# A two-layer hybrid diffusion step on one core: order of transposes, products, weight loads and output tiles changed

## The chip, the cores and the metric

One core of a Trainium2 chip runs the whole step. TensorE (PE, with its weight loads shown as PEld) multiplies and transposes, VectorE (DVE), ScalarE (ACT) and GpSimd (POOL) do the rest, and SyncE (SP) issues most of the transfers; ACT issues some. Each engine takes its own instructions in order. The metric is the device time of one execution in microseconds, lower is better.

## The reference: what is computed

Two layers are applied to 256 context tokens and to 1024 latent tokens of width 1024. A layer normalises and modulates its input, projects it to 4400 columns, runs three groups of heads over it in both directions, and projects the result back:

```python
h = _rmsnorm(x, g) * (1.0 + scale) + shift
proj = jnp.einsum('bld,de->ble', h, w_in)
# A: mLSTM, 4 heads x 128      ya = sigmoid(ao) * (ha_f + flip(ha_b))
# B: retention, 4 heads x 64   yb = hb_f + flip(hb_b)
# C: gated linear attention    yc = hc_f + flip(hc_b)
y = jnp.concatenate([_head_rms(ya), _head_rms(yb), _head_rms(yc)], axis=-1)
y = y * hn_g * jax.nn.silu(jnp.concatenate([az, bz, cz], axis=-1))
out = jnp.einsum('ble,ed->bld', y, w_out)
x = x + gate * out
```

Shift, scale and gate come from a modulation, a product of a vector with w_ada. Latent scans start from cached states; the final states of the context scans are returned as well as both outputs.

## The kernel before

The 1280 tokens are ten chunks of 128, in three blocks of 256, 512 and 512 tokens (BLK). Every large product is done in three terms: inputs and weights are each split in a high part, ACT's cast (L516), and a low part, DVE's subtraction (L517), and hi*hi, hi*lo and lo*hi are accumulated, 24 matmuls for a block or a chunk. The split inputs stay in hA (blocks 0 and 1) and hB (block 2).

Weights are loaded on SP's queue into a ring of two raw tiles (L526, in load), and split into rings of three hi and three lo tiles. Loads and splits are traced ahead of their use by a scheduling priority (AHEAD); load adds an order behind the fourth last entry of a list of past projections (uses). A feature-major projection (mm_fm, L566) takes one tile of 512 KB and goes over the three blocks; a token-major one (mm_tm, L581) takes two tiles and goes over the chunks in pairs. Results go through two PSUM banks (pj). A layer has 22 feature-major projections (14 of ORDER, eight gate paths) and nine token-major ones (five of ORDER, four of the output). gates (L702) is a product of its own, with three weight pieces of 304 columns (gates_w); the third piece of layer 0 is loaded into a tile of the arena f.

The order of PE's work is written by a planner (Weave). Each stage is a generator, which yields a gap, a condition and the tiles it needs; the planner takes the first that is ready by its own clock and costs, and chains PE's instructions in that order. So a PE instruction that waits holds back all behind it. Threads run in the order of rank: the mixers, then the modulations, then the projections of ORDER, then the fillers (gate paths, gate_z). The other engines' order comes from a scheduler that simulates times.

The parts that the change and the prediction touch:

- late_setup and decay_setup (L318 to L342) load masks, gate biases, initial maxima and the retention decays (L335, L338), and take a log-sigmoid of the decays (L310 to L316) before the planned part begins. load_x (L458) loads tokens.
- modulation_late computes one quarter of a modulation: eight products (L418), ACT's copy of the row (L422), a fold (L427) 4 us later by the planner's clock.
- group_c: for five pairs of chunks it transposes keys (L1007), multiplies them with the values into one bank, two products for each chunk (L1015), and updates states with DVE (L987, L991) after each chunk's products.
- head_a, one mLSTM head: for pairs of chunks it loads rows (rows_in, L1485) and prepares weights (L1494 to L1497); in each step come products (L1510, L1512), then the next pair's scores (L1503) with DVE's multiply (L1504) in the first half of the bank `other`, then transposes of the output of two steps earlier (L1551) in its second half, and the head's arithmetic (L1518 to L1574). Steps are 5 us apart by the planner.
- gate_z multiplies a group's output by its gate path: it loads a tile of yd (L1591), projects (L566), and writes yd back (L1597), through wk, a ring of three tiles.
- fillers: when the last gate path is to be done, two f tiles take block 0 of the seven other output tiles (L1627). The entry z of ORDER then waits for the gate paths and, in layer 0, for the modulations (early).
- out_proj: for all three blocks it loads tiles of yd through wk (L1693), splits them (L1694, L1695), allocates ten xt tiles, transposes the gate vector (L1701), writes it to DRAM (grow) and reads it back broadcast (L1709), loads the ten x chunks (L1712), and runs four token-major products, whose evictions (L1725) take a wk tile each.

The arena f has 12 tiles. `edge` with SCHED_ONLY and `issue_after` order instructions without a semaphore.

Of the kernel before, what the change touches and what calls it, by code (L numbers as in the profile page):

```python
# [9 lines left out]
F32 = mybir.dt.float32  # L10
# [81 lines left out]
def hybrid_step(ctx: ExitStack, tc: tile.TileContext, A, O):  # L92
# [225 lines left out]
    def late_setup():  # L318
        t = rw()
        sync.dma_start(t, A["cst"][:, K_MF:K_MF + 4 * P])  # L320
        dve.tensor_copy(masks, t)
        dve.tensor_scalar(later, t[:, 0:P], 0.0, None, ALU.is_lt)
# [8 lines left out]
    def decay_setup():  # L331
# [5 lines left out]
        for t in range(2):  # L337
            sync.dma_start(lg[64 * t:64 * t + 64, 16:24], rl2[t:t + 1, :].to_broadcast([64, 8]),  # L338
                           allow_slow_non_contiguous=True)

# [65 lines left out]
    def modulation_late(l, c0):  # L406
# [17 lines left out]
        yield wait(4.0, mx=1)  # L424
# [25 lines left out]

    def load_x(b):
# [59 lines left out]
    def split(raw, parts=1, cols=1024):  # L511
        hi, lo = hi_ring(), lo_ring()
        n = cols // parts
        for i in range(0, cols, n):
            e = slice(i, i + n)
            act.copy(hi[:, e], raw[:, e])  # L516
            dve.tensor_tensor(lo[:, e], raw[:, e], hi[:, e].bitcast(F32), ALU.subtract)  # L517
        return hi, lo

    anchor, uses = [None], []  # L520

    def load(*dmas):

        with ExitStack() if anchor[0] is None else tc.issue_after(anchor[0]):
            for out, src in dmas:
                i = sync.dma_start(out, src)  # L526
                if len(uses) > 4:
                    edge(i.ins, uses[-4], mybir.DependencyReason.SCHED_ONLY)

    def w_fm(src, c0):  # L530

        with tc.high_priority(offset=AHEAD):
            raw = raw_ring()
            load((v3(raw, P), src[:, c0:c0 + P].rearrange("(k p) n -> p k n", p=P)))
            hi, lo = split(raw)
        return v3(hi, P), v3(lo, P)

    def w_tm(src, c0, ks=range(KT)):

        out = []  # L540
        for g in range(2):
            with tc.high_priority(offset=AHEAD):
                raw = raw_ring()
                i = 0
                while i < 4:
                    k = ks[4 * g + i]
                    n = 1
                    while i + n < 4 and ks[4 * g + i + n] == k + n:
                        n += 1
                    load((v3(raw, 256)[:, i:i + n, :],  # L550
                          src[k * P:(k + n) * P, c0:c0 + 256].rearrange("(k p) n -> p k n", p=P)))
                    i += n
# [1305 lines left out]
```

## Time and profile before

| | us |
|---|---|
| median of 2 timed runs | 1773.28 (1768.79 to 1777.78) |
| the profiled execution's own time | 1782.73 |
| its span, first to last instruction | 1780.9 |
| PE busy | 1607.7 (90%), 11126 matmuls |
| DVE busy | 889.8 (50%) |
| ACT busy | 608.1 (34%) |
| POOL busy | 116.5 (7%) |
| moved by DMA | 239.64 MB, 135 GB/s on average |

An engine's busy time is the union of its instructions. Idle time of PE is put down to what ended it. The mean granted clock of PE is 0.949 of full speed; it is either 1 (2.4 GHz) or 0.5 (1.2 GHz).

### The profile page before, as it was taken

What the parts mean: (1) busy time and instruction counts of PE and PEld (TensorE: products, weight loads), DVE (VectorE), ACT (ScalarE), POOL (GpSimd) and SP (SyncE); (2) the same over time, 40 slices, a digit from 0 to 9 for tenths busy, and PEclk for the clock granted to TensorE, in tenths of its full rate; (3) what the DMA queues carried; (4) which work ended last, traced back from release to release, by engine and by line L of the source; (5) the groups of instructions that cost most, each with busy time, mean ns of one, the idle gap of its engine ahead of it and who ended that gap; (6) DMA issues with size and microseconds to landing.
All of it is one profiled execution on the core that took longest, in us unless ns stands there. A gap on an engine that the chain in (4) does not pass through costs nothing.

```text
span 1780.9 us, 28991 instructions
## 1 busy us (share of the span) xinstructions
PE 1607.7 (90%) x11126; PEld 1455.8 (82%) x11126; DVE 889.8 (50%) x2216; ACT 608.1 (34%) x1553; POOL 116.5 (7%) x195
## 2 busy tenths in 40 slices
PE   6698899999999877897999988999999989888897
PEld 3577689998988766786999868999899877776897
DVE  3449444572354454544354785347505455554545
ACT  5454213112433332233255631221224333323323
POOL 1100010101000000000011000110100000000001
PEclk8799999999999988997999999999999999898799
DMA  8134326424647466553131331271244546566303
GB/s 315 53 113 126 100 99 219 119 63 133 187 139 217 134 190 208 175 174 119 38 113 48 111 105 58 95 237 51 77 144 141 164 124 209 164 192 195 96 13 121
DMA packets 217409, 239.64 MB, mean 135 GB/s; under 512 B 23901, under 2 KB 171645, under 8 KB 217261
## 3 DMA queue, kind: packets, MB, share of 16 engines
q1 hardware_dynamic: 179392, 195.68, 36.2%
q10 hardware_dynamic: 37868, 42.01, 6.8%
q8 instruction: 89, 1.46, 0.3%
q14 instruction: 60, 0.48, 0.1%
HBM read 173.01 MB, written 64.55 MB: 133 GB/s over the span
## 4 chain that ended last, share of the span: by engine, by line
PE 41%; DMA 7%; DVE 5%; ACT 2%; issue 1%; SPq 1%; POOL 0%; ACTq 0%; POOLq 0%; DVEq 0%
PE pj L581 18%; PE pj L566 14%; DMA yd<-wk 2%; DMA wk<-yd 2%; PE pj L702 2%; DMA rw<-wrow 1%; DMA rw<-rrow 1%; PE mx L1449 1%; DMA f<-sp 1%; PE mx L1510 1%; PE mx L1512 1%; DVE f L659 1%; DVE lo L517 1%; PE mx L1315 1%; PE mx L1078 0%
## 5 line engine op out<-in xcount | busy, mean ns | idle before, releaser
L566 PE MATMUL pj<-hA,hi 128*128 128x256 f32 (+1 forms) x1408 | 364.5, 351 | 10.9 <-ACT wk L594 10.7
L581 PE MATMUL pj<-hi,hA 128*128 128x256 f32 x1728 | 338.0, 296 | 23.0 <-ACT hA L1694 12.9
L581 PEld LDWEIGHTS pj<-hi,hA 128*128 128x128 f32 x1728 | 283.0, 200 | 30.6 <-ACT hA L1694 15.7
L566 PEld LDWEIGHTS pj<-hA,hi 128*128 128x128 f32 x1408 | 245.3, 196 | 43.1 <-ACT wk L594 11.1
L581 PE MATMUL pj<-lo,hA 128*128 128x256 f32 x864 | 251.6, 291 | 0.0
L566 PE MATMUL pj<-hA,lo 128*128 128x512 f32 (+1 forms) x704 | 242.3, 344 | 0.0
L566 PE MATMUL pj<-hB,hi 128*128 128x512 f32 x704 | 229.4, 408 | 11.4 <-DVE wk L1595 10.5
L581 PE MATMUL pj<-hi,hB 128*128 128x256 f32 x1152 | 212.2, 285 | 0.0
L517 DVE TENSOR_TENSOR lo<-raw,hi 128x256 fp32r<-128x256 f32 (+2 forms) x193 | 116.4, 624 | 153.2 <-ACT hi L516 134.9
L581 PEld LDWEIGHTS pj<-hi,hB 128*128 128x128 f32 x1152 | 179.0, 191 | 1.6 <-issue 0.8
L581 PEld LDWEIGHTS pj<-lo,hA 128*128 128x128 f32 x864 | 173.3, 201 | 0.0
L566 PEld LDWEIGHTS pj<-hB,hi 128*128 128x128 f32 x704 | 132.7, 195 | 41.4 <-DVE wk L1595 11.3
L581 PE MATMUL pj<-lo,hB 128*128 128x256 f32 x576 | 162.9, 283 | 0.0
L516 ACT CAST hi<-raw 128x256 fp32r<-128x256 f32 (+2 forms) x193 | 104.5, 565 | 139.6 <-PE pj L566 98.6
L566 PEld LDWEIGHTS pj<-hA,lo 128*128 128x128 f32 x704 | 137.2, 195 | 15.9
L566 PE MATMUL pj<-hB,lo 128*128 128x512 f32 x352 | 141.0, 401 | 0.0
L581 PEld LDWEIGHTS pj<-lo,hB 128*128 128x128 f32 x576 | 110.2, 191 | 0.0
L444 ACT ACTIVATE rw<-f 128x256 bf16<-128x256 f32 (+1 forms) x90 | 43.4, 484 | 123.1 <-DVE f L1728 121.5
L592 ACT COPY wk<-pj 128x256 f32<-128x256 f32 (+1 forms) x102 | 40.9, 431 | 126.5 <-PE pj L581 63.8
L566 PEld LDWEIGHTS pj<-hB,lo 128*128 128x128 f32 x352 | 68.1, 193 | 15.4
L1725 DVE TENSOR_TENSOR wk<-pj,f 128x512 f32<-128x512 f32 (+1 forms) x45 | 28.4, 632 | 95.5 <-PE pj L581 95.5
L1441 ACT ACTIVATE sm<-mx,ccol 128x128 f32<-128x128 f32 x144 | 45.9, 367 | 65.0 <-PE mx L1438 63.9
(271 smaller groups left out, 2426.8 us busy)
## 6 DMA issues: line engine op xcount, KB each, us to landing
raw<-in_w_in_dram SPq DMA_DIRECT2D x64, 512.0 KB
f<-in_w_ada_dram SPq DMA_DIRECT2D x48, 512.0 KB
f<-sp SPq DMA_DIRECT2D x36, 640.0 KB
sp<-wk ACTq DMA_DIRECT2D x128, 128.0 KB
wk<-yd SPq DMA_DIRECT2D x64, 256.0 KB
sp<-wk ACTq DMA_DIRECT2D x56, 256.0 KB
rw<-rrow SPq DMA_DIRECT2D x40, 256.0 KB
rw<-wrow SPq DMA_DIRECT2D x40, 256.0 KB
```

The source lines that it names most:

```text
L444: act.activation(rw().bitcast(BF16)[:, 0:x.shape[1]], x, AF.Square, accum_out=out)
L516: act.copy(hi[:, e], raw[:, e])
L517: dve.tensor_tensor(lo[:, e], raw[:, e], hi[:, e].bitcast(F32), ALU.subtract)
L566: end = pe.matmul(ps[:, :n], lhsT=w[wi][:, k, :], rhs=hblk(xi, k, b), start=(i == 0), stop=(i == 23))
L581: end = pe.matmul(pv[:, u, :], lhsT=hchunk(xi, k, c), rhs=w[e // 4][wi][:, e % 4, :], start=(i == 0), stop=(i == 23))
L592: act.copy(out, ps)
L659: dve.tensor_tensor_scan(o, ones[r, 0:n], i, 0.0, ALU.mult, ALU.add)
L702: end = pe.matmul(ps, lhsT=hchunk(xi, k, c), rhs=w[k // 3][wi][:, k % 3, :], start=(i == 0), stop=(i == 23))
L1315: pe.matmul(banks[u][:, (2 * d + r) * P:(2 * d + r + 1) * P], lhsT=last[d][:, (2 * u + r) * P:(2 * u + r + 1) * P], rhs=vv[r][:, c, 0:P], ...
L1441: act.activation(ks[:, d * P:(d + 1) * P], pk, AF.Copy, scale=ccol[:, c, 2 + d, hd:hd + 1])
L1449: pe.matmul(U[d], lhsT=ks[:, d * P:(d + 1) * P], rhs=v[:, c, :], start=True, stop=True)
L1725: dve.tensor_tensor(t, pv, row.unsqueeze(1).to_broadcast([P, len(cs), 256]), ALU.mult)
```

## The change

late_setup becomes a thread of the planner that takes in decay_setup: its loads come after the last x load, and masks and log-sigmoid 20 and 40 us later. The modulation's fold waits 8 us for 4. load makes raw tile, load and split in one; loads are ordered behind the end of the projection two back (for the last gate piece, one back), splits behind the middle of the projection before; token-major tiles are split in two parts for four; the third gate piece uses the raw ring. In group_c all four products of a step come before the updates; in head_a the transposes come before the scores. In fillers the last gate path waits for 12 free f tiles and, in layer 0, for the modulations, and then out_tiles loads blocks 0 and 1 of the seven output tiles, the gate vectors and six x chunks; out_proj loads the rest.

```diff
     def late_setup():
-        t = rw()
+        yield wait()
+        t = rw.take()
         sync.dma_start(t, A["cst"][:, K_MF:K_MF + 4 * P])
-        dve.tensor_copy(masks, t)
-        dve.tensor_scalar(later, t[:, 0:P], 0.0, None, ALU.is_lt)
...
-    def decay_setup():
...
+        yield wait(20.0)
+        dve.tensor_copy(masks, t)
+        dve.tensor_scalar(later, t[:, 0:P], 0.0, None, ALU.is_lt)
+        rw.give(t)
+        yield wait(20.0)
         lt = sm()
         log_sigmoid(lg, lt[:, 0:24], lt[:, 24:48])
...
-        yield wait(4.0, mx=1)
+        yield wait(8.0, mx=1)
...
-            sync.dma_start(t, tokens(A["x_prompt"], A["x_sample"], c0 + j))
+            xl.append(sync.dma_start(t, tokens(A["x_prompt"], A["x_sample"], c0 + j)))
...
+    def load(src, *parts, behind=2, n=1):
         hi, lo = hi_ring(), lo_ring()
+        raw = raw_ring()
+        with tc.high_priority(offset=AHEAD):
+            with ExitStack() if anchor[0] is None else tc.issue_after(anchor[0]):
+                for view, rows in parts:
+                    i = sync.dma_start(view(raw), rows)
+                    if len(ends) >= behind:
+                        edge(i.ins, ends[-behind], mybir.DependencyReason.SCHED_ONLY)
+            for j in range(0, src, src // n):
+                c = slice(j, j + src // n)
+                for i in (act.copy(hi[:, c], raw[:, c]),
+                          dve.tensor_tensor(lo[:, c], raw[:, c], hi[:, c].bitcast(F32), ALU.subtract)):
+                    if mids and behind > 1:
+                        edge(i.ins, mids[-1], mybir.DependencyReason.SCHED_ONLY)
         return hi, lo
...
-            for out, src in dmas:
-                i = sync.dma_start(out, src)
-                if len(uses) > 4:
-                    edge(i.ins, uses[-4], mybir.DependencyReason.SCHED_ONLY)
...
-        if b == 2:
-            uses.append(end.ins)
+        if b:
+            (ends if b == 2 else mids).append(end.ins)
...
-        if cs[-1] == NCH - 1:
-            uses.extend([end.ins] * 2)
+        if cs[-1] in (5, NCH - 1):
+            (mids if cs[-1] == 5 else ends).append(end.ins)
...
-            raw = f5(1024) if l == 0 and k == 6 else raw_ring()
...
+            hi, lo = load(n * 304, *parts, behind=1 if k == 6 else 2)
...
                 for u, c in enumerate(order[i - 1]):
+                    for p in range(2):
+                        h = slice(256 * u + p * P, 256 * u + (p + 1) * P)
+                        pe.matmul(bank[:, h], lhsT=last[:, h], rhs=v3(vt[p], 129)[:, c, 0:P], start=True, stop=True)
+                for u, c in enumerate(order[i - 1]):
                     U = bank[:, 256 * u:256 * u + 256]
...
-            if ahead:
-                scores(c0 + 2, ahead[0], other[:, 0:256])
             out = before.pop(0) if len(before) == 2 or before and c0 >= NCH else None
             if out is not None:
                 was, pt = out[1], other[:, 256:512]
                 for u in range(2):
                     pe.transpose(pt[:, u * P:(u + 1) * P], out[0][:, u * P:(u + 1) * P], ident)
+            if ahead:
+                scores(c0 + 2, ahead[0], other[:, 0:256])
...
-                    yield wait(0, f=2)
...
+                    yield wait(0, cond=early, f=12, mx=1, sm=1)
+                    e["y"] = out_tiles(l, [kt for kt in range(KT) if kt not in tiles_of[g]])
...
-                yield wait(0, cond=lambda: not left and not busy and "y" in e and early())
+                yield wait(0, cond=lambda: not left and not busy and "y" in e)
...
+    def out_tiles(l, kts):
         xt = [f5(1280) for _ in range(NCH)]
+        first = [f5(1280) for _ in range(2)]
+        y = {}
+        for i, kt in enumerate(kts):
+            y[0, kt] = first[i // 5][:, 256 * (i % 5):256 * (i % 5) + 256]
+            y[1, kt] = xt[6 + i // 2][:, 512 * (i % 2):512 * (i % 2) + 512]
+        for b, kt in sorted(y):
+            t0, n = BLK[b]
+            sync.dma_start(y[b, kt], yd[kt, :, t0:t0 + n])
...
-        sync.dma_start(grow, gr)
+        act.dma_start(grow, gr)
...
+        for c in range(6):
+            x_in(l, c, xt[c])
+        return xt, first, gate, y
+
+    def out_proj(l, tiles, normed):
+
+        xt, first, gate, y = tiles
...
+        f5.give(*first)
+        for c in range(6, NCH):
+            x_in(l, c, xt[c])
...
-            with tc.issue_after(adas[-1].ins):
-                late_setup()
...
+            weave.add(late_setup())
+            with tc.issue_after(xl[-1].ins):
+                weave.visit(weave.threads[0])
```

## Rows read from the trace of the kernel before

**Rows 1.** Busy us by stretch: length, PE, PEld, DVE, ACT, POOL; clock; DMA share; GB/s

```profile
0.00:80.00 80.00, 47.93 (x274) 32.70 (x275) 34.02 (x63) 43.32 (x80) 12.52 (x31) 0.81 0.60 205
...
160.00:240.00 80.00, 63.56 (x387) 53.01 (x386) 48.27 (x114) 22.49 (x44) 3.55 (x3) 0.94 0.32 98
...
500.00:790.00 290.00, 251.41 (x1556) 219.41 (x1555) 139.42 (x433) 95.22 (x281) 17.01 (x36) 0.92 0.58 177
790.00:830.00 40.00, 27.56 (x138) 23.84 (x137) 17.43 (x30) 13.85 (x31) 0.20 (x1) 0.70 0.57 168
...
1380.00:1630.00 250.00, 215.85 (x1302) 191.01 (x1301) 132.39 (x405) 86.15 (x264) 15.56 (x29) 0.94 0.56 173
1630.00:1672.00 42.00, 31.46 (x160) 27.48 (x159) 18.75 (x34) 13.92 (x30) 0.00 (x0) 0.72 0.51 154
```

**Rows 2.** Waits of PE: who waited for whom, us in total, times, longest

```profile
PE mx L1551 <- DVE rw L1504: 42.8, 16, 7.1
PE pj L581 <- ACT hA L1694: 12.9, 10, 2.4
PE pj L702 <- DVE lo L517: 12.6, 2, 12.1
...
PE mx L427 <- ACT wk L422: 11.0, 1, 11.0
PE pj L566 <- DVE wk L1595: 10.5, 3, 5.4
PE mx L1015 <- DVE f L991: 9.3, 8, 2.2
...
PE pj L581 <- DVE wk L1725: 8.1, 2, 4.2
```

**Rows 3.** Timeline at the start, 40 to 64 us: start, us, engine, line

```profile
46.73 1.65 SPq L526 DMA_DIRECT2D f<-in_w_in_dram  x2
...
48.94 1.42 SPq L338 DMA_DIRECT2D lg<-in_ret_decay_logit_dram  x2
...
50.59 0.88 PE L702 MATMUL pj<-hi,hA 128*128 128x304 f32 x2 [5.07 <-ACT hi L516]
61.65 0.18 DVE L310 SCALAR_TENSOR_TENSOR sm<-lg 128x24 f32<-128x24 f32 x1 [11.64 <-issue]
...
63.60 0.62 PE L702 MATMUL pj<-lo,hA 128*128 128x304 f32 x1 [12.13 <-DVE lo L517]
```

**Rows 4.** Timeline of a head stage, 583 to 606 us

```profile
587.68 0.69 DVE L1497 TENSOR_TENSOR rw<-rw,f 128x512 f32<-128x512 f32 x1 [3.48 <-DMA rw<-wrow]
...
589.09 0.69 PE L1551 MATMUL mx<-cst,sm 128*128 128x128 f32 x2 [4.96 <-DVE rw L1504]
...
600.40 0.44 PE L1551 MATMUL mx<-cst,sm 128*128 128x128 f32 x2 [0.86 <-DVE rw L1504]
```

**Rows 5.** Busy time by stretch, behind the long wait

```profile
589.00:594.50 5.50, 5.41 (x17) 4.55 (x18) 2.00 (x8) 2.22 (x9) 0.70 (x1) 0.50 0.35 111
```

**Rows 6.** Timeline of the output projection's start, layer 0: PE, SP, DVE

```profile
793.77 0.48 PE L581 MATMUL pj<-hi,hA 128*128 128x256 f32 x2
...
805.27 17.19 SPq L1693 DMA_DIRECT2D wk<-yd  x11
...
839.08 0.69 DVE L1725 TENSOR_TENSOR wk<-pj,f 128x512 f32<-128x512 f32 x1 [4.27 <-PE pj L581]
...
844.84 0.69 DVE L1725 TENSOR_TENSOR wk<-pj,f 128x512 f32<-128x512 f32 x1 [0.69 <-PE pj L581]
```

**Rows 7.** Line L427, all its instructions: duration min/median/max, first and last start

```profile
L427 PE MATMUL mx<-fold,wk x64: 165/251/371, 132.3 to 697.1; 128*128 128x2 f32 x64
```

**Rows 8.** Waits of SP's queue, the first line

```profile
SPq L526 <- DVE lo L517: 361.5, 34, 40.3
```

**Rows 9.** Timeline, 620 to 637 us: a weight tile's split on ACT and DVE

```profile
626.16 1.03 ACT L516 CAST hi<-raw 128x1024 fp32r<-128x1024 f32 x1
...
627.24 1.22 DVE L517 TENSOR_TENSOR lo<-raw,hi 128x1024 fp32r<-128x1024 f32 x1
```

More of the change, by code (lines that the diff above doesn't have):

```diff
@@ L449, in rstd @@
         pool.tensor_tensor(ss, ss, mhalf[:, 0:ss.shape[1]], ALU.pow)
+    xl = []
     def load_x(b):
@@ L508, in norm_thread @@
         done.add(b)
-    def split(raw, parts=1, cols=1024):
+    anchor, mids, ends = [None], [], []
+    def load(src, *parts, behind=2, n=1):
         hi, lo = hi_ring(), lo_ring()
[L513 to L517, printed above, removed]
-        return hi, lo
-    anchor, uses = [None], []
-    def load(*dmas):
-        with ExitStack() if anchor[0] is None else tc.issue_after(anchor[0]):
-            for out, src in dmas:
-                i = sync.dma_start(out, src)
-                if len(uses) > 4:
-                    edge(i.ins, uses[-4], mybir.DependencyReason.SCHED_ONLY)
+        raw = raw_ring()
[11 more added lines that the diff above has]
+                        edge(i.ins, mids[-1], mybir.DependencyReason.SCHED_ONLY)
+        return hi, lo
     def w_fm(src, c0):
[L532 to L535, printed above, removed]
+        hi, lo = load(1024, (lambda t: v3(t, P), src[:, c0:c0 + P].rearrange("(k p) n -> p k n", p=P)))
         return v3(hi, P), v3(lo, P)
@@ L541, in w_tm @@
         for g in range(2):
[L542 to L552, printed above, removed]
-                hi, lo = split(raw, 4)
+            parts, i = [], 0
+            while i < 4:
+                k = ks[4 * g + i]
+                n = 1
+                while i + n < 4 and ks[4 * g + i + n] == k + n:
+                    n += 1
+                parts.append((lambda t, i=i, n=n: v3(t, 256)[:, i:i + n, :],
+                              src[k * P:(k + n) * P, c0:c0 + 256].rearrange("(k p) n -> p k n", p=P)))
+                i += n
+            hi, lo = load(1024, *parts, n=2)
             out.append((v3(hi, 256), v3(lo, 256)))
@@ L667, in gates_w @@
             n = min(3, KT - k)
-            raw = f5(1024) if l == 0 and k == 6 else raw_ring()
-            r = v3(raw[:, 0:912], 304)[:, 0:n, :]
-            load(*[(r[:, :, d:d + m], src[:, k:k + n, c0:c0 + m])
-                   for d, c0, m in ((0, C_CV, 256), (256, C_AG, 16), (272, C_LR, 32))])
-            hi, lo = split(raw, 1, n * 304)
-            if l == 0 and k == 6:
-                f5.give(raw)
+            parts = [(lambda t, d=d, m=m: v3(t[:, 0:912], 304)[:, 0:n, d:d + m], src[:, k:k + n, c0:c0 + m])
+                     for d, c0, m in ((0, C_CV, 256), (256, C_AG, 16), (272, C_LR, 32))]
+            hi, lo = load(n * 304, *parts, behind=1 if k == 6 else 2)
             out.append((v3(hi[:, 0:912], 304), v3(lo[:, 0:912], 304)))
@@ L715, in gates @@
             pend.append((c, gt))
-        uses.extend([end.ins] * 3)
+            if c in (5, NCH - 1):
+                (mids if c == 5 else ends).append(end.ins)
         def rest():
@@ L1784, in program @@
         if not general:
-            with tc.issue_after(adas[-1].ins):
-                late_setup()
-        if not general:
-            with tc.issue_after(adas[-1].ins):
-                decay_setup()
+            weave.add(late_setup())
+            with tc.issue_after(xl[-1].ins):
+                weave.visit(weave.threads[0])
         anchor[0] = None if general else adas[-1].ins
-        uses.clear()
+        for marks in (mids, ends):
+            marks.clear()
         normed, prepared = set(), set()
```

42 lines of the change are left out of this document (15 added, 27 removed).

## The prediction, as put on record before the result was known

> **What bounds the kernel now.** I read the stretches first, then the waits of PE, then the timeline around each long wait, and last SP's waits. The stretches [rows 1] show that PE is the bound, but not everywhere alike: from 0 to 80 us it is busy for 47.9 us at a granted clock of 0.81, from 160 to 240 for 63.6, in the mLSTM head stages (500 to 790 and 1380 to 1630) for 251.4 of 290 and 215.9 of 250, and at the two starts of the output projection (790 to 830, 1630 to 1672) for 27.6 of 40 and 31.5 of 42. These six hold 144 of the 173 us that PE is without work (1780.9 - 1607.7), and lose more where its clock fell from 2.4 to 1.2 GHz. So an edit is worth what it takes out of such stretches; DVE or ACT time saved elsewhere is worth nothing.
>
> The waits of PE [rows 2] say what ends the idle time: 42.8 us in 16 waits of the head transposes (L1551) for the DVE multiply of the scores (L1504), 12.6 us of the gate products (L702) for the split of their weights, 13 us and 8 us of the output projection (L581) for its input and for its evictions, 11 us of one modulation fold (L427), 10.5 us of gate paths (L566) for DVE, 9.3 us of GLA state products (L1015).
>
> **The change, part by part.** The sum is made against the profiled execution's own 1782.7 us, 9.4 above the median of the timed runs (1773.3); I take the same difference off that median.
>
> *Start (late_setup, gates_w).* The timeline shows DVE standing for 11.6 us before the first instruction of the log-sigmoid (L310), which needs the decay table whose last two transfers SP issues at 48.9 (L338); the split of the third piece of the gate weights (L517) stands behind it in DVE's queue, so PE waits 12.1 us at 63.6 [rows 3]. The change puts that log-sigmoid two waits of 20 us later, in a thread, so nothing stands before the split. Before that, PE waited 5.07 us for the third piece itself, which SP issued only at 46.7, behind small tables that now come after the last x load [rows 3]. New: the third piece uses the ring of two raw buffers and must wait for the first piece's split. From its issue to the products that need it took 3.9 us before (46.7 to 50.6), and PE was there at 45.5 (50.59 - 5.07). I take 13 of the 17.2 us; bounds 4 (the ring delays the piece) and 19 (all, and some of the half-clock time).
>
> *Head transposes ahead of the scores.* PE takes its instructions in the order of the weave. Today scores, their DVE multiply and then the transposes use one bank, so PE stands until DVE is through, with all its other work queued behind. One long wait of eight: the multiply is late because DVE waits 3.5 us for a row transfer (L1497), and PE stands 4.96 us; one short of eight: 0.86 us, the bare multiply [rows 4]. With the transposes first, PE needs nothing new: they read a tile of two steps earlier. The short ones (8 x 0.86 = 6.9) go. The long ones hold 42.8 - 6.9 = 35.9; DVE stays late, and the next PE instruction that needs it is the product of the following step, placed 5 us behind by the planner, so part comes back. I take 60%, 21.5 us. After the shown wait PE worked 5.4 us at a granted clock of 0.50 [rows 5], so 2.7 lost; about two of the six longest are worth that, 5 us. Together 33; bounds 7 (short ones only) and 59 (42.8 and six times 2.7).
>
> *GLA products ahead of what reads their bank.* The four products of a step no longer wait between chunks for DVE to read the first chunk's half. 9.3 us [rows 2]; I take 7, since DVE's updates then decide when the next step's state is there. Bounds 0 and 9.3, or 12 with clock.
>
> *Output tiles early (out_tiles).* The output projection of layer 0 starts at 793.8; its pairs of chunks come 5.76 us apart once it runs, and the fifth is evicted at 844.84 [rows 6]. Five pairs are 28.8 us, so the start loses 844.8 - 793.8 - 28.8 = 22.2 us. Layer 1 repeats it (10.5 us idle and clock 0.72 beside 12.4 and 0.70 [rows 1]). The cause: 17 tiles of block 0 to 2 go through three wk buffers, and the first eviction's tile, in the same ring, comes behind them; SP gives 11 of these loads 17.2 us, 1.56 each [rows 6]. After it, 10 tiles go through the ring (the last gate's for blocks 0 and 1, eight of block 2); the first eviction takes the buffer of the eighth. 8 x 1.56 = 12.5 us, from about 795, is 807.5, and a split of about 1.5 after it. PE wants the third pair's bank at 793.8 + 11.5 = 805.3. So 4 us of wait are left, 2 of half clock, and some 4 for the last four x chunks (2 MB), which move into this moment: 10 of 22. The gain is 12 for each layer, 24; bounds 6 and 44. The wait for 12 free tiles costs nothing, I think: the last head has given all its tiles when the last gate starts, and the last modulation fold is at 697.1 [rows 7]. The gate vectors' write on ACT's queue is one issue. Its cover is the last gate's three blocks; without it, PE would wait for 14 loads.
>
> *Modulation fold 4 us later.* PE waited 11 us once [rows 2] for ACT's copy of the row; with 4 us more work ahead, 3 go; bounds 0 and 4.
>
> *Loads and splits tied to steps.* Today a weight load is traced so far ahead that it stands at the head of SP's queue until its raw buffer is split: 361.5 us in 34 waits, up to 40 [rows 8], and row loads, gate tiles and x loads stand behind it. Tied to the end of the projection two back, the load comes when its buffer is free. Rows then come in time more often (that part is in the 60% above), and some of the 10.5 us of L566 for DVE go: 4 us. In cost: the split now follows the middle of the projection before. It takes 1.03 us on ACT and 1.22 on DVE [rows 9]; left to the end are two pairs in token-major projections, 11.5 us, and 24 products of 512 columns in the others, at twice 0.12 us (5.76 / 48) about 5.8 us. That covers it by 3.5 us if the data has landed. Bounds: 15 gained, and the fifth case below.
>
> The ties are orders without a semaphore and may change nothing; that would cost the 4 us. Retention ahead of the heads, as the title has it, has no line in the diff: nothing.
>
> Sum: 13 + 33 + 7 + 24 + 3 + 4 = 84 us. 1782.7 - 84 = 1698.7 for a profiled execution, 1773.3 - 84 = 1689 for the median.
>
> A page speaks against the tied loads. The Trainium skill, "DMA: Bandwidth & Descriptors", Rules for kernel authors, says to issue a transfer early and wait for it late, so that its fixed cost overlaps with compute. No row here shows a weight load that PE waits for after the start, and SP's 361.5 us show that an early place in the queue was not an early landing; by the rule the time would be that of the fifth case.
>
> **The rivals.**
> 1. *The wait moves on.* DVE stays late by what the rows cost it, and PE stands at the next step's products instead of the transposes. For it: DVE is idle half the time and yet late, so latency rules, not load [rows 1, 4]. Against it: the filler products between. Then the head term is 7: 84 - 26 = 58, 1715 us.
> 2. *Waits move on everywhere.* As 1, and the wk ring still holds the output projection (6) and the raw ring the start (4): 4 + 7 + 7 + 6 = 24, 1749 us, which is no difference by 2%.
> 3. *More than forecast.* With SP's queue free, rows land in time and the long head waits go whole, with their clock: 59 in place of 33, and 10 more of the output projection: 120, 1653 us.
> 4. *It doesn't do what it says*: the ties change no order. 80 in place of 84: 1693, inside the forecast.
> 5. *The weights come late (slower).* A split that starts only at the end of the projection before makes PE stand for 1.03 + 1.22, about 2.3 us, at each of 62 projections (in the two layers, 44 feature-major and 18 token-major): 143 us against 84, 1832. It decides from 84 / 62 = 1.35 us each. For it: cover of one projection in place of two or three, and ACT and DVE take splits in their turn. Against it: 3.5 us of cover and free buffers.
>
> **How the numbers follow.** Forecast (with case 4) 49%, case 1 23%, case 2 9%, case 3 14%, case 5 5%. 2% of the median is 35 us, about what a measurement of this kernel tells from no change: faster is below 1738, slower above 1809. Forecast, 1 and 3 hold 86%, less a little for a forecast that misses: 0.85; within 2%: 0.10; slower: 0.05. The range from 1640 to 1745 takes in cases 1, 3 and the nearer half of 2, and the bounds of the unknown terms except all at one end.
>
> **What would show it.** Right: no wait of L1551 for L1504 and of L1015 for L991; at the start no idle DVE before L310 and the gate products running on by about 47 us; fifth eviction of the output projection some 39 us after its start in place of 51; fewer SP waits of weight loads for L517, fewer DVE waits for the rows. Wrong: a new wait of like size at L1510 or L1503 for DVE (case 1), of L581 for the wk ring (case 2), or many waits of L566 and L581 for L516 and L517 (case 5).

## The result, and the profile after

The changed kernel takes 1677.79 us (median of 2 runs, 1677.57 to 1678.01), against 1773.28: ratio 0.946, 95% interval 0.936 to 0.957. Beside the experiments, in five runs, it took 1679.5 us with a ratio of 0.944 (0.943 to 0.946), 98.8 us of 1777.7. The forecast was 84 us and 1689. Two profiles of this same kernel span 1676.1 and 1680.0 us, so differences of 4 us between single profiles mean nothing.

Lines have moved: the head transposes L1551 are now L1547, the scores' multiply L1504 is L1502, scores L1503 are L1501, products L1510 are L1508, the rows' multiply L1497 is L1495, L566 is L567, L581 is L582, L702 is L699, the splits L516 and L517 are L530 and L531, the weight load L526 is L525, the evictions L1725 are L1735, the loads and splits of yd in the output projection L1693, L1694 are L1717, L1718, the fold L427 is L429, the state products L1015 are L1012, and in the gate paths the load L1591, DVE's multiply L1595 and the write L1597 are L1589, L1593 and L1595. In the runs below, lines behind an edit shift by a few more; tiles and operations tell which they are.

The first lines of the page after:

```profile
span 1676.1 us, 28715 instructions
...
PE 1573.1 (94%) x11126; PEld 1430.8 (85%) x11126; DVE 882.7 (53%) x2144; ACT 593.5 (35%) x1481; POOL 116.8 (7%) x195
```

The matmuls are as many as before, yet PE is busy for 34.6 us less (1607.7 - 1573.1), because more of them run at the higher clock: its mean is 0.973, before 0.949. PE's time without work fell from 173.2 to 103.0 us (1676.1 - 1573.1). So of the 104.8 us between the two profiles two thirds are waits that went and one third is clock that came back with them.

The stretches after; each stands for one of [rows 1], moved to where its stage now lies:

```profile
0.00:80.00 80.00, 59.15 (x362) 42.79 (x363) 35.26 (x61) 44.84 (x95) 13.15 (x35) 0.94 0.64 218
160.00:240.00 80.00, 75.03 (x604) 65.95 (x606) 41.43 (x101) 22.03 (x40) 5.89 (x4) 0.98 0.32 97
470.00:740.00 270.00, 251.06 (x1601) 218.36 (x1600) 148.53 (x451) 96.97 (x287) 17.77 (x37) 0.96 0.65 199
740.00:782.00 42.00, 33.09 (x248) 32.39 (x247) 16.33 (x29) 12.49 (x31) 0.00 (x0) 0.88 0.43 143
1285.00:1535.00 250.00, 234.89 (x1494) 211.03 (x1493) 148.74 (x451) 96.84 (x289) 16.64 (x30) 0.97 0.59 182
1535.00:1580.00 45.00, 34.54 (x255) 33.81 (x254) 20.18 (x38) 12.48 (x31) 0.00 (x0) 0.85 0.46 148
```

At the start PE now issues 362 matmuls in 80 us in place of 274. In 270 us the first head stage has as much PE time as in 290 before, 251 us, and issues 1601 matmuls in it for 1556; the second has 234.9 of 250 us, before 215.9. The output projection's starts rose to a clock of 0.88 and 0.85, the lowest that is left in this table.

The waits of PE after, to set against [rows 2]:

```profile
PE pj L582 <- ACT hA L1718: 14.9, 2, 8.7
PE pj L567 <- DVE wk L1593: 14.4, 3, 7.9
...
PE pj L699 <- ACT hi L530: 5.9, 1, 5.9
...
PE pj L582 <- DVE wk L1735: 4.4, 2, 2.7
...
PE mx L1508 <- DVE ti L1518: 3.6, 1, 3.6
...
PE mx L1508 <- DVE rw L1502: 2.7, 3, 2.1
...
PE pj L567 <- DVE lo L531: 2.4, 2, 1.7
...
PE mx L1508 <- DVE rw L1520: 2.0, 2, 1.4
```

The wait of 42.8 us for the scores' multiply is gone, as are those of the fold (11.0) and of the state products (9.3), and the 12.1 us that the gate products waited for their split at the start. The gate paths' wait for DVE (L567), of which the forecast took 4 us off, is larger: 14.4 us for 10.5. What came is small at the heads (L1508), but the output projection has a new one of another kind: not ten short waits for its input as in [rows 2], but one long wait in each layer. The timeline around the first of the two, from four engines:

```profile
737.05 0.41 SPq L1595 DMA_DIRECT2D yd<-wk  x1
737.56 1.91 SPq L1679 DMA_DIRECT2D f<-in_x_sample_dram  x3
740.13 0.33 SPq L1595 DMA_DIRECT2D yd<-wk  x1
742.63 0.33 SPq L1589 DMA_DIRECT2D wk<-yd  x1
747.02 0.32 SPq L1717 DMA_DIRECT2D wk<-yd  x1
```

```profile
740.59 0.40 PE L582 MATMUL pj<-hi,hA 128*128 128x256 f32 x2
...
749.51 1.04 PE L582 MATMUL pj<-hi,hA 128*128 128x256 f32 x2 [6.25 <-ACT hA L1718]
```

```profile
749.05 0.41 ACT L1718 CAST hA<-wk 128x256 fp32r<-128x256 f32 x1 [7.66 <-DMA wk<-yd]
```

```profile
747.71 0.75 DVE L1594 SCALAR_TENSOR_TENSOR wk<-wk,hgh,wk 128x512 f32<-128x512 f32 x1 [5.59 <-DMA wk<-yd]
...
781.81 0.69 DVE L1735 TENSOR_TENSOR wk<-pj,f 128x512 f32<-128x512 f32 x1 [0.21 <-PE pj L582]
```

The write of the last gate path's block 0 to yd is issued at 737.05 (L1595), but it is read back only at 747.0 (L1717), and PE has reached the rows of that tile at 743.3 (749.51 - 6.25). SP's waits in the same profile say what the read back stood for:

```profile
SPq L1717 <- DMA yd<-wk: 10.3, 3, 6.0
```

4.0 of these 10.3 us end at 747.0, 6.0 at the same place in layer 1. They are not for block 0. The ring wk has three tiles, and in the kernel's order block 2's load (L1589) takes the one that block 0 was written from, and the read back (L1717) the one of block 1. SP, which waits with L1589 for the write of block 0, goes on at 742.6, so block 0 was through by then; with L1717 it waits until the write of block 1, issued at 740.13, is through as well. In layer 1 block 0 was through by 1531.5, and PE came to its rows at 1538.4 and still waited 8.7 us. So most of the new wait, 4.0 of 6.25 us and 6.0 of 8.7, is a wait for a tile of the ring.

The fifth eviction is at 781.81: 781.81 - 740.59 - 28.8 = 12.4 us are lost at this start, in layer 1 14.4 (1579.02 - 1535.77 - 28.8), against 22.2 by [rows 6].

### The profile page after: what moved, and what is told of

The parts are those of the page before. It is cut to its first block, busy times and chain, and to the rows that moved or that the text cites. A ratio compares the mean times of both kernels' runs of the same rounds, so it can differ in the third digit from the quotient of the medians.

```text
span 1676.1 us, 28715 instructions
## 1 busy us (share of the span) xinstructions
PE 1573.1 (94%) x11126; PEld 1430.8 (85%) x11126; DVE 882.7 (53%) x2144; ACT 593.5 (35%) x1481; POOL 116.8 (7%) x195
## 4 chain that ended last, share of the span: by engine, by line
PE 69%; DMA 12%; DVE 10%; ACT 4%; issue 2%; SPq 2%; POOL 0%; ACTq 0%; POOLq 0%; DVEq 0%
PE pj L582 28%; PE pj L567 21%; PE pj L699 4%; DMA yd<-wk 4%; DMA rw<-rrow 2%; DMA wk<-yd 2%; PE mx L1447 2%; PE mx L1508 1%; DMA rw<-wrow 1%; DMA f<-sp 1%; PE mx L1510 1%; DVE f L660 1%; PE mx L1313 1%; DVE lo L531 1%; PE mx L1076 1%
## 5 line engine op out<-in xcount | busy, mean ns | idle before, releaser
L567 PE MATMUL pj<-hA,hi 128*128 128x256 f32 (+1 forms) x1408 | 362.2, 349 | 17.2 <-DVE wk L1593 12.6
L582 PE MATMUL pj<-hi,hA 128*128 128x256 f32 x1728 | 323.1, 288 | 19.4 <-ACT hA L1718 14.9
L582 PEld LDWEIGHTS pj<-hi,hA 128*128 128x128 f32 x1728 | 274.0, 195 | 22.5 <-ACT hA L1718 15.3
L567 PEld LDWEIGHTS pj<-hA,hi 128*128 128x128 f32 x1408 | 243.1, 195 | 48.4 <-DVE wk L1593 13.2
L582 PE MATMUL pj<-lo,hA 128*128 128x256 f32 x864 | 246.7, 286 | 0.0
L567 PE MATMUL pj<-hA,lo 128*128 128x512 f32 (+1 forms) x704 | 241.5, 343 | 2.4 <-DVE lo L531 2.4
L567 PE MATMUL pj<-hB,hi 128*128 128x512 f32 x704 | 222.4, 397 | 1.8 <-DVE wk L1593 1.8
L582 PE MATMUL pj<-hi,hB 128*128 128x256 f32 x1152 | 212.0, 285 | 0.3 <-ACT wk L593 0.3
L582 PEld LDWEIGHTS pj<-hi,hB 128*128 128x128 f32 x1152 | 179.1, 192 | 2.0 <-issue 0.8
L582 PEld LDWEIGHTS pj<-lo,hA 128*128 128x128 f32 x864 | 168.1, 195 | 0.0
L582 PE MATMUL pj<-lo,hB 128*128 128x256 f32 x576 | 162.9, 283 | 0.0
L567 PEld LDWEIGHTS pj<-hB,hi 128*128 128x128 f32 x704 | 128.3, 188 | 29.6 <-issue 2.5
L567 PEld LDWEIGHTS pj<-hA,lo 128*128 128x128 f32 x704 | 136.7, 194 | 18.2 <-DVE lo L531 2.8
L531 DVE TENSOR_TENSOR lo<-raw,hi 128x512 fp32r<-128x512 f32 (+3 forms) x122 | 106.9, 902 | 84.5 <-ACT hi L530 73.8
L567 PE MATMUL pj<-hB,lo 128*128 128x512 f32 x352 | 137.7, 391 | 0.0
L582 PEld LDWEIGHTS pj<-lo,hB 128*128 128x128 f32 x576 | 110.3, 191 | 0.0
L530 ACT CAST hi<-raw 128x512 fp32r<-128x512 f32 (+3 forms) x122 | 91.5, 785 | 31.4 <-PE pj L582 7.9
L446 ACT ACTIVATE rw<-f 128x256 bf16<-128x256 f32 (+1 forms) x90 | 43.5, 484 | 120.1 <-DVE f L1738 118.3
L567 PEld LDWEIGHTS pj<-hB,lo 128*128 128x128 f32 x352 | 66.1, 188 | 14.5
L1508 PE MATMUL mx<-f,rw 128*128 128x129 f32 x320 | 63.3, 284 | 8.3 <-DVE ti L1518 3.6
L1735 DVE TENSOR_TENSOR wk<-pj,f 128x512 f32<-128x512 f32 (+1 forms) x45 | 28.4, 632 | 78.7 <-PE pj L582 78.7
```

The source lines that it names most:

```text
L446: act.activation(rw().bitcast(BF16)[:, 0:x.shape[1]], x, AF.Square, accum_out=out)
L530: for i in (act.copy(hi[:, c], raw[:, c]), dve.tensor_tensor(lo[:, c], raw[:, c], hi[:, c].bitcast(F32), ALU.subtract)):
L531: dve.tensor_tensor(lo[:, c], raw[:, c], hi[:, c].bitcast(F32), ALU.subtract)):
L567: end = pe.matmul(ps[:, :n], lhsT=w[wi][:, k, :], rhs=hblk(xi, k, b), start=(i == 0), stop=(i == 23))
L582: end = pe.matmul(pv[:, u, :], lhsT=hchunk(xi, k, c), rhs=w[e // 4][wi][:, e % 4, :], start=(i == 0), stop=(i == 23))
L1508: pe.matmul(po[:, d, :], lhsT=r4[:, d, u, :], rhs=v[:, c, :], start=True, stop=not inter)
```

## The experiments

What an undone part costs is read from ratios: its ratio less 0.9444 (the changed kernel, with five runs), times 1777. Such a difference is good to about 5 us either way.

**The head transposes, undone.**

```diff
+            if ahead:
+                scores(c0 + 2, ahead[0], other[:, 0:256])
             out = before.pop(0) if len(before) == 2 or before and c0 >= NCH else None
...
-            if ahead:
-                scores(c0 + 2, ahead[0], other[:, 0:256])
```

> The changed kernel with the head's scores put back ahead of the transposes, all else as changed. Theory 1 (each part of the change frees PE where its own wait stood): the waits of the transposes for the scores' multiply come back, 16 of them and some 35 to 45 us, and with the half-clock time behind the long ones the kernel takes 1710 to 1725 us. Theory 2 (the tied loads did it, by letting the row transfers land in time): only the bare multiplies come back, 16 x 0.86 = 14 us, 1685 to 1695 us.

Measured 1716.65 us, ratio 0.967 (0.964 to 0.970): 41 us. Its waits of PE:

```profile
PE mx L1549 <- DVE rw L1502: 41.5, 16, 6.4
```

The wait returns with the same count and nearly the same length as in [rows 2], although loads, splits and output tiles are those of the changed kernel. It hangs on this order and on nothing else of the change.

**The head transposes alone**, in the kernel before: the reverse of the diff above, and nothing else.

> The kernel before with one part of the change alone: in head_a the transposes of the output of two steps earlier come ahead of the next scores; nothing else is changed. Undoing this part in the changed kernel cost 38.9 us (1716.7 against 1677.8). Theory 1, the part works by itself: the waits of the transposes for the scores' multiply (42.8 us in 16) go here too, and it gains as much as there, 33 to 45 us: 1732 to 1744. Theory 2, it needs the freer SP queue: with weight loads still at the head of that queue, rows land late, DVE is late, and the wait moves on to the products of the next step: 7 to 20 us gained, 1757 to 1770, with new waits of L1510 and L1503 for DVE of over 15 us in all.

Measured 1733.33 us, ratio 0.976 (0.973 to 0.980): 42 us gained (0.0235 x 1776), as much as undoing it cost. In its waits of PE the 42.8 us are gone, and this is all that stands for the heads' products in their place:

```profile
PE mx L1510 <- DVE rw L1504: 1.9, 1, 1.9
PE mx L1510 <- DVE rw L1522: 1.9, 3, 1.1
PE mx L1510 <- DVE ti L1520: 0.9, 1, 0.9
```

4.7 us, of which the kernel before had 1.3 (L1522 and L1520, 0.9 and 0.4). SP's queue is as full as before, 362.2 us of weight loads waiting for L517 [rows 8]. Theory 2, which needs a freer queue, falls.

**The ties, undone**: loads again ordered behind the fourth last entry of one list, splits behind nothing, token-major tiles in four parts; raw tile, load and split stay in one.

```diff
-                    if len(ends) >= behind:
-                        edge(i.ins, ends[-behind], mybir.DependencyReason.SCHED_ONLY)
+                    if len(uses) > 4:
+                        edge(i.ins, uses[-4], mybir.DependencyReason.SCHED_ONLY)
...
-                    if mids and behind > 1:
-                        edge(i.ins, mids[-1], mybir.DependencyReason.SCHED_ONLY)
```

> The changed kernel with weight loads ordered as before (fourth last entry of the list of uses), splits without an order and in four parts; the third gate piece stays in the raw ring. Theory 1: the ties are worth little, 0 to 8 us, 1678 to 1686 us. Theory 2: SP's queue fills again, rows come late, 1700 to 1720 us. Rival to both (the tied splits cost more than they give): faster than 1674 us.

Measured 1676.3 us, ratio 0.944 (0.942 to 0.946): no difference from the changed kernel. SP's waits say that the order did change, in this run and then in the changed kernel:

```profile
SPq L525 <- DVE lo L531: 399.8, 42, 38.6
```

```profile
SPq L525 <- DVE lo L531: 262.1, 32, 20.8
```

That is 138 us less in this row, but the queue is hardly freer: summed over all rows of this view SP waits 1326.3 us here and 1316.4 in the changed kernel, where weight loads wait longer for writes to DRAM (sp<-wk, 116.5 us for 59.2). And the rows of the heads come sooner without the ties. DVE's multiply of the rows in this run:

```profile
L1492 DVE TENSOR_TENSOR rw<-rw,f 128x512 f32<-128x512 f32 x40 | 27.5, 687 | 20.3 <-DMA rw<-wrow 20.3
```

It waits 20.3 us for them, in the changed kernel 33.3. None of this shows in the time.

**The output tiles, undone**: seven tiles of block 0 early as before, the rest through wk, gate vectors and x in the output projection.

```diff
-                    yield wait(0, cond=early, f=12, mx=1, sm=1)
-                    e["y"] = out_tiles(l, [kt for kt in range(KT) if kt not in tiles_of[g]])
+                    yield wait(0, f=2)
+                    e["y"] = y = [f5() for _ in range(2)], {}
```

> The changed kernel with the output projection's tiles loaded as before (block 0 early, the rest through the wk ring). By the stretches of the two traces the two starts lost 22.2 and 21.6 us before and lose 12.4 and 14.4 us now: 17 us come back, 1692 to 1698 us. Rival (early loads crowd the last gate path's transfers and cost as much there): 1678 to 1684 us.

Measured 1703.58 us, ratio 0.959 (0.957 to 0.961): 26 us. The start and the fifth eviction of layer 0 in its timeline (PE, DVE):

```profile
742.45 0.48 PE L582 MATMUL pj<-hi,hA 128*128 128x256 f32 x2
...
793.64 0.69 DVE L1723 TENSOR_TENSOR wk<-pj,f 128x512 f32<-128x512 f32 x1 [0.21 <-PE pj L582]
```

793.64 - 742.45 - 28.8 = 22.4 us lost, the 22.2 of [rows 6] again. The fifth eviction comes 11.8 us behind that of the changed kernel, and in layer 1 24.1 behind (1603.11 against 1579.02): 12 for each layer. 18 of these 24 us are lost at the two starts (22.4 - 12.4 and 22.6 - 14.4), as the expected 17 had it. The other 6 come earlier, since the starts themselves lie 1.9 and 4.1 us later; PE waits 18.6 us for DVE at the gate paths in this run (L567 for L1593), 14.4 in the changed kernel.

**The start, undone**: the tables and the log-sigmoid in one go ahead of the planned part; the third gate piece stays in the raw ring.

```diff
-            weave.add(late_setup())
-            with tc.issue_after(xl[-1].ins):
-                weave.visit(weave.threads[0])
+            with tc.issue_after(adas[-1].ins):
+                for _ in late_setup():
+                    pass
```

> The changed kernel with masks and log-sigmoid back ahead of the planned part, in one go behind the last modulation load; the third gate piece stays in the raw ring. Theory: DVE stands for the decay table again and the gate products wait some 12 us, 1686 to 1694 us. Rival (the gate products are held by their third piece in any case): within 3 us of 1678.

Measured 1693.18 us, ratio 0.954 (0.952 to 0.956): 17 us by ratios, 14 by medians. In its timeline DVE stands before the log-sigmoid as in [rows 3], and PE waits 13.44 us for the high half of the split and then 3.38 for the low one (DVE, then PE):

```profile
56.71 0.18 DVE L310 SCALAR_TENSOR_TENSOR sm<-lg 128x24 f32<-128x24 f32 x1 [12.04 <-DMA lg<-in_ret_decay_logit_dram]
```

```profile
58.44 0.88 PE L699 MATMUL pj<-hi,hA 128*128 128x304 f32 x2 [13.44 <-ACT hi L530]
```

**The state products, undone.**

```diff
                 for u, c in enumerate(order[i - 1]):
-                    for p in range(2):
-                        h = slice(256 * u + p * P, 256 * u + (p + 1) * P)
-                        pe.matmul(bank[:, h], lhsT=last[:, h], rhs=v3(vt[p], 129)[:, c, 0:P], start=True, stop=True)
-                for u, c in enumerate(order[i - 1]):
                     U = bank[:, 256 * u:256 * u + 256]
+                    for p in range(2):
+                        h = slice(p * P, (p + 1) * P)
+                        pe.matmul(U[:, h], lhsT=last[:, 256 * u + p * P:256 * u + (p + 1) * P],
+                                  rhs=v3(vt[p], 129)[:, c, 0:P], start=True, stop=True)
```

> The changed kernel with one part undone: in group_c the four products of a step are again written chunk by chunk, each pair followed by DVE's updates of its chunk. Theory 1, the forecast's step: PE's waits of the state products for the update (9.3 us before, none after) come back, less what the next step's wait takes over: 7 us, bounds 0 and 12, so 1680 to 1690, likeliest 1685 beside 1677.8. Theory 2, what DVE needs is only moved to the next read of the state: no difference, 1676 to 1680. Under theory 1 the trace has again about eight waits of the second chunk's products for DVE, 7 to 10 us in all; under theory 2 it has them too, but other waits are shorter by as much.

Measured 1691.87 us, ratio 0.952 (0.950 to 0.954): 13 us. The group of these products, in this run and in the changed kernel:

```profile
L1013 PE MATMUL mx<-f,rw 128*128 128x128 f32 x80 | 13.2, 288 | 9.1 <-DVE f L989 6.8 <-ACT sta L1018 2.3
```

```profile
L1012 PE MATMUL mx<-f,rw 128*128 128x128 f32 x80 | 10.6, 275 | 0.0
```

Theory 1 holds, with a size a little above its bounds: there are 9.1 us of waits here, for ACT's copies from the bank as well as for DVE's updates. And PE is busy for 8 to 9 us more (1580.9 us, in the two profiles of the changed kernel 1573.1 and 1571.5), so the clock is as large a part of the 13 as the waits.

**The fold, undone.**

```diff
-        yield wait(8.0, mx=1)
+        yield wait(4.0, mx=1)
```

> The changed kernel with one part undone: the fold of a modulation quarter follows its row's copy by 4 us of the planner's clock again, not 8. Theory 1, the forecast's step: a wait for 4 us more work ahead is 3 us cheaper, at most 4: 1681 (1678 to 1682). Theory 2: the wait of 11.0 us came once, where ACT was far behind the planner's clock, and with the order of everything else changed ACT is not late there: no difference, 1677 to 1679, and no wait of the fold for ACT above 2 us. Theory 3: the whole wait returns with the clock it costs: 1688 to 1694.

Measured 1682.96 us, ratio 0.949 (0.946 to 0.951): 3.5 us by medians, 7 by ratios, not far outside what the comparison can tell from nothing. The wait of 11.0 us returns once, behind ACT's copy of the row (PE, then ACT):

```profile
597.30 1.87 PE L429 MATMUL mx<-fold,wk 128*128 128x2 f32 x8 [10.96 <-ACT wk L424]
```

```profile
593.04 0.60 ACT L1592 ACTIVATE wk<-pj 128x512 f32<-128x512 f32 x1 [8.02 <-DMA yd<-wk]
596.66 0.58 ACT L424 COPY wk<-mx 128x512 f32<-128x512 f32 x1 [3.02 <-DMA yd<-wk]
```

ACT is late because it waits twice for a tile of wk, whose content is still being written to yd. Theory 2 falls, since the wait came; but less than theory 3's 10 to 16 us of it reach the end. In part other waits are shorter in its place: the gate paths' for DVE is 9.0 us in this run, in the changed kernel 14.4.

**The x loads first**: the six loads that the output tiles' step issues come first in it.

```diff
         xt = [f5(1280) for _ in range(NCH)]
+        for c in range(6):
+            x_in(l, c, xt[c])
...
-        for c in range(6):
-            x_in(l, c, xt[c])
```

> The changed kernel with one thing moved: the six loads of x chunks that the output tiles' step issues come first in it, ahead of the 14 loads of y tiles and of the gate vectors. The changed kernel has one new wait in each layer, 6.3 and 8.7 us, of the output projection's fourth pair of chunks or so for block 0 of the last gate's tile, which DVE writes to DRAM and SP reads back while 3 MB of x chunks are on their way. Theory 1, these x loads crowd that round trip: issued some 15 us earlier, they are through by then, and the waits shrink to under 2 us each: 1664 to 1672. Theory 2, the round trip is late by itself (DVE waits for its own load before it multiplies): the waits stay within 2 us, 1675 to 1680. Theory 3: the y tiles behind 3 MB of x now come late: new waits for them, 1682 or more.

Measured 1681.95 us, ratio 0.947 (0.944 to 0.950), not faster. The wait stands as it was:

```profile
PE pj L582 <- ACT hA L1718: 16.3, 2, 9.3
```

That the x loads crowd the round trip was a story that fitted the timeline, and it falls: theory 2.

**The changed kernel once more**, beside the three runs that follow here.

> The changed kernel itself once more, beside the runs of this call, so that effects below 1% are read on one chip: 1674 to 1682, ratio to the kernel before 0.942 to 0.947. If the undone parts are independent, what they cost (heads 39, output tiles 26, start 15, state products 14, fold 5, ties 0, about 99) should come near to its whole gain of some 98 us; under a rival in which the parts cover for each other (one wait taking another's place) the whole gain would be clearly less or more than that sum.

Measured 1679.51 us, ratio 0.944 (0.943 to 0.946). The undone parts sum to 41 + 26 + 17 + 13 + 7 - 1 = 103 us by ratios and 88 by medians (37.1 + 24.1 + 13.7 + 12.4 + 3.5 - 3.2, each less 1679.5), around the whole gain of 98.8. They are independent, as far as a sum can tell whose terms are each good to some 5 us.

**The third gate piece ahead of the small tables.**

```diff
-            with tc.issue_after(xl[-1].ins):
+            with tc.issue_after(wl[-1].ins):
```

Here wl collects the loads of the gate weights.

> The changed kernel with one order moved: the small tables of the first thread (masks, biases, initial maxima, decays) are ordered behind the last load of the three gate weight pieces, not behind the last x load. In the changed kernel SP issues the third piece at 45.3, behind these tables, and PE waits 5.9 us for it. Theory 1, the queue is what delays it: issued some 5 us earlier, the wait goes or shrinks below 2 us, and the time is 4 to 7 us less, 1671 to 1674 beside 1677.8. Theory 2, the ring delays it (the raw tile is free only after the first piece's split): same wait within 1 us, 1676 to 1680.

Measured 1679.80 us, ratio 0.945 (0.944 to 0.947): nothing gained. SP's waits from 30 to 50 us, and then SP's queue, ACT and PE in its timeline:

```profile
SPq L525 <- DVE lo L532: 3.7, 2, 3.2
```

```profile
33.76 4.11 SPq L462 DMA_DIRECT2D f<-in_x_sample_dram  x4
41.20 2.43 SPq L525 DMA_DIRECT2D raw<-in_w_in_dram  x4
```

```profile
47.32 1.07 ACT L446 ACTIVATE rw<-f 128x1024 bf16<-128x1024 f32 x1
...
48.36 0.71 ACT L531 CAST hi<-raw 128x608 fp32r<-128x608 f32 x1
```

```profile
49.12 0.87 PE L700 MATMUL pj<-hi,hA 128*128 128x304 f32 x2 [3.68 <-ACT hi L531]
50.97 0.62 PE L700 MATMUL pj<-lo,hA 128*128 128x304 f32 x1 [0.97 <-DVE lo L532]
```

With the tables out of the way, SP is through with x at 37.9 and then waits 3.2 us for the first piece's split: now the ring holds the piece. It is issued 4.1 us earlier (41.2, not 45.3) and cast only 2.0 us earlier (48.36 against 50.41 in the changed kernel, where the cast waited for its DMA): ACT has no idle time before the cast, but works through squares of x (L446) until then. PE's wait falls from 5.9 to 4.65 us (3.68 + 0.97), and a gain of that size is below what can be seen. So both theories are half right: the tables were the first of three things in line, the ring and ACT's queue the next.

**The last gate path kept on chip**: its result is split at once into the halves that the output projection reads; the write to yd and the read back fall away for this tile. The computation is whole.

```diff
             dve.scalar_tensor_tensor(yv, th, hgh[:, 8 * l + kt:8 * l + kt + 1], yv, ALU.mult, ALU.mult)
-            sync.dma_start(yd[kt, :, t0:t0 + n], yv)
+            if last:
+                hi, lo = hblk(0, kt, b), hblk(1, kt, b)
+                act.copy(hi, yv)
+                dve.tensor_tensor(lo, yv, hi.bitcast(F32), ALU.subtract)
+            else:
+                sync.dma_start(yd[kt, :, t0:t0 + n], yv)
...
             for k in ks:
+                if k == kept:
+                    continue
```

> The changed kernel with the last gate path's result split straight from its tile into the halves that the output projection reads, for all three blocks, where it was written to DRAM and read back through the ring wk. Nothing of the computation is left out. The loads of x alone, moved earlier, left the new wait of 16 us in two as it was. Theory 1, that round trip is the wait (DVE waits 5.6 us for a tile load that stands behind a write to DRAM, then the write and the read back follow): both waits go, with some half clock behind them: 12 to 20 us, 1658 to 1666. Theory 2, PE is then held at the next product for something else (the ten tiles of blocks 1 and 2 in the ring wk, the first eviction): 0 to 6 us, 1672 to 1678, with a new wait of L582 for ACT or DVE of like size.

Measured 1666.04 us, ratio 0.937 (0.935 to 0.939): 14 us faster than the changed kernel (0.0079 x 1777). In its waits of PE the one for ACT is gone, and the one for the evictions is larger by 3.6 (4.4 in the changed kernel):

```profile
PE pj L582 <- DVE wk L1744: 8.0, 2, 4.3
```

Start and fifth eviction of layer 0 (PE, DVE):

```profile
743.66 0.40 PE L582 MATMUL pj<-hi,hA 128*128 128x256 f32 x2
...
778.54 0.69 DVE L1744 TENSOR_TENSOR wk<-pj,f 128x512 f32<-128x512 f32 x1 [0.21 <-PE pj L582]
```

6.1 us are lost here (778.54 - 743.66 - 28.8) and 5.6 in layer 1, of 12.4 and 14.4: the write and the read back were the wait, theory 1, and a part of it moved on to the evictions, as theory 2 had it. The run doesn't separate the way through DRAM from the ring: the read back's need of a tile of wk went with it. A fourth tile in the ring, or another place for this one read, was not tried.

**Both at once.**

> Both at once: the small tables behind the gate weights, and the last gate path's result kept on chip. The start and the output projection lie far apart, so the two should add: what each gains by itself, within 3 us; by theories 1 of both 1652 to 1662, by theories 2 of both no gain, 1674 to 1680.

Measured 1665.64 us, ratio 0.937 (0.935 to 0.939): the same as the last one alone, as the third piece gives nothing. Keeping the last gate path on chip beats both kernels, by 14 us and by 113 (0.0635 x 1777.7).

## Why the prediction was right, and where its terms were off

The forecast was a sum of local waits, and the local waits went: 98.8 us against 84, with all parts but the ties of the sign that was forecast. Its terms, by the runs:

*Start: 13, measured 14 to 17.* The mechanism held: no DVE stall before the split, no wait of PE for it above 0.7 us. The sign that was named, gate products running on by about 47 us, came at 51.2: the third piece was still late by 5.9 us, behind small tables, and behind these the ring waits, as was feared, and ACT's queue. The 13 of 17.2 allowed for that.

*Head transposes: 33, measured 41 and 42.* The sign held: no wait for L1504's successor. The step that was off is "I take 60%". It rested on DVE staying late by the rows and on the next step's products paying for it. DVE did stay late. Its group of the rows' multiply, before and after:

```profile
L1497 DVE TENSOR_TENSOR rw<-rw,f 128x512 f32<-128x512 f32 x40 | 27.6, 690 | 26.4 <-DMA rw<-wrow 26.2
```

```profile
L1495 DVE TENSOR_TENSOR rw<-rw,f 128x512 f32<-128x512 f32 x40 | 27.6, 689 | 33.3 <-DMA rw<-wrow 33.3
```

It waits for rows longer than before, 33.3 us; the sign "fewer DVE waits for the rows" was wrong, and so was the thought that the ties would bring the rows in time (with the ties undone it waits 20.3). But what follows is covered. Without the bank's reading in front of it, PE goes on with filler products, and the multiply is through before PE comes to the step's products. One such step of the changed kernel (DVE, then PE):

```profile
520.12 0.69 DVE L1495 TENSOR_TENSOR rw<-rw,f 128x512 f32<-128x512 f32 x1 [3.55 <-DMA rw<-wrow]
...
526.59 0.69 DVE L1502 TENSOR_TENSOR rw<-rw,mx 128x512 f32<-128x512 f32 x1 [1.50 <-PE mx L1501]
```

```profile
532.52 0.60 PE L1508 MATMUL mx<-f,rw 128*128 128x129 f32 x4
```

From the multiply's end at 527.3 to the products at 532.5 there are 5.2 us to spare, in a stretch where a row came 3.55 us late. So 3.4 of the 42.8 us came back with this part alone (4.7 - 1.3), and 7.0 in the changed kernel (8.3 for L1508 in all, less 1.3), not 40%: 28.9 of the 35.9 us of the long waits stay away in the changed kernel (42.8 - 6.9 - 7.0), 80% and not 60. The clock was more than the 5 us taken, too: PE is busy for 7 to 9 us more where this part is undone (1580.3 against 1573.1 and 1571.5), and for 11.0 less with this part alone (1607.7 - 1596.7). Case 1, the wait that moves on, needed the opposite and fell with both head runs.

*State products: 7, measured 13.* The size was off. The term took the wait for DVE only; 2.3 us for ACT's copies from the same bank go with it (9.1 in all in the run that undoes it), and its 7 had no clock in it, where PE's busy time fell by 8 to 9 us; 160 to 240 us rose from 0.94 to 0.98.

*Output tiles: 24, measured 26.* That the sums agree is in part luck. Where the forecast looked, between the start and the fifth eviction, 41.2 and 43.3 us are left of 51.1 and 50.4: 17 us went there, not 24, and most of the rest came before the starts, where no step of the sum had it. What is left, 12.4 and 14.4 where 10 were forecast, was put down to the ring's loads and to the x chunks that move there. Moving x gave nothing. The ring it was for the most part, but not by its loads: the read back of the last gate's tile stood for a tile of the ring that was still being written to DRAM. Keeping that tile on chip gave half of the loss back. Its write and read back were in no step of the sum.

*Fold: 3, measured 3.5 to 7.* All 11 us of the wait went, not 3, and why 4 us more work ahead did that is not shown; yet less than the wait came back as time.

*Ties: 4, measured 0.* This step failed. It read SP's waits of weight loads as a queue that holds rows and gate tiles back. Those waits did fall (399.8 to 262.1 us), but SP waited for other things instead (1326.3 and 1316.4 us in all); rows came later by the ties and not earlier (20.3 us of DVE's waits without them, 33.3 with them); and the wait of L566 for DVE, 10.5 us of which 4 were to go, is 13.4 without the ties and 14.4 with them. Case 4 had the right price for another reason: the ties changed the order, and the order was worth nothing. Case 5 did not come either, as PE's waits for the split after are 2.4 us in all at the feature-major projections. So the rule of the Trainium skill cited in the prediction ("DMA: Bandwidth & Descriptors", Rules for kernel authors: issue early, wait late) is neither broken nor confirmed by these loads: later issue cost nothing here, and earlier issue gains nothing, and the one load that PE did wait for, the third gate piece, gained nothing from going out 4.1 us earlier, since ACT was busy when it came.

*Cases 2 and 3.* Waits did not move on everywhere (1749), though the ring wk, which case 2 names, is behind most of what is left at the output projection. Case 3 had the head waits go whole, which is near to what was seen, but for a reason (rows in time) that the rows refute, and with 10 us more at the output projection that did not come.

## What to carry to other kernels

If an instruction of an engine that works in order waits only because another engine still reads the same bank, put it ahead of what that engine reads. With some 5 us of independent work in front of the next true need, four fifths of the long waits went here, and clock with them, although the other engine stayed as late. Queue waits of SP are no price by themselves: 138 us less in one row changed nothing here, since the queue waited elsewhere, and PE's waits named hardly any of these loads (2.4 us for their splits). And after early loads are in place, look for the one tile that can't be loaded early, because it is still being computed: see which buffer its read back will wait for, and if its consumer is on the same chip, try to keep it there.

## What was not expected of the hardware

A tile that goes through DRAM can come back late for another tile's sake: in the changed kernel the write of 128 x 256 was issued at 737.05 and through by 742.6, and the read back took 2.0 us (747.02 to 749.05), but between the two SP stood 4.0 us for a buffer whose own write to DRAM took from 740.13 to 747.0. And clock is a third of a gain that was counted in waits: 34.6 us less busy time for the same 11126 matmuls.
